# Joining the scan steps of a hybrid mixer block into fewer, longer visits between its projection products

## The chip, the cores and the metric

One Trainium2 chip, one core of it. The metric is device time in microseconds (us) of the one launch. TensorE (PE) multiplies, VectorE (DVE) and ScalarE (ACT) read and write PSUM and SBUF, GpSimd (POOL) reads and writes SBUF, and DMA queues are fed by SP, ACT and POOL.

## The reference

One layer over 512 latent tokens and 256 context tokens of width 2048, all in float32. Both streams are normalised, modulated by a condition, and multiplied by one wide input projection. Its columns feed three groups of heads: 6 heads of a bidirectional gated DeltaNet (GDN), a Hyena group of long convolutions, and 6 heads of a bidirectional mLSTM. The two scans, cut to their steps:

```python
# GDN, per chunk: dec = exp(g_i - g_j) below the diagonal
kk  = k @ k.T;  a_mat = I + tril(beta * kk * dec);  a_qk = (q @ k.T) * dec
def step(s):
    u = u_t - w @ s                       # the triangular solve is folded into u_t, w
    o = (q * exp(g)) @ s + a_qk @ u
    s = exp(g_end) * s + k_end.T @ u
# mLSTM, per chunk
p   = exp(d_log - m_i) * (q @ k.T)
num = w_inter * (q @ C) + p @ v;  den = w_inter * (q @ n) + p.sum()
h   = num / max(|den|, exp(-m_i));  C = dec * C + (w * k).T @ v
# every group: norm, gate, one output projection, residual, final norm
```

Each scan runs forwards and backwards; the latent scan starts from the state that the context scan leaves.

## The kernel before

The kernel works on tiles of 128 tokens: 2 context tiles and 4 latent ones, NT = 6 in all, NC_ = 2, NL = 4, and d = 0, 1 for the two directions. It has three stretches. The first loads, normalises and modulates the inputs and makes the Hyena filters. The middle one does the input projection, 64 column tiles of 128, with the scans between. The last does the long convolutions and the output projection.

The middle stretch is ordered by a planner written in Python, `weave` (from line 808). A *filling* generator yields one step of a projection product at a time, `product` (L396): three matmuls of 128x512 for the latent tokens (L404, L405, L409) and, for column tiles that need the context, three of 128x256 (L407, L408, L411). Weights are split into a high and a low part by ACT (L274) and DVE (L275), a few pieces ahead. Four *chains*, which are generators too, hold the rest: `gdn` (prepare and scan head after head), `ml_scans`, `gates_row` (a vector-matrix product on DVE, with its weights loaded by SP, L1535 and L1541) and, at the end, `convs`. A chain yields a pair: the planner's cost of the PE work that it has just issued, and a delay after which it is due again. Whenever a chain is due by the planner's clock, it gets a step; if none is due, the next product step is issued and the clock moves by 0.65 or 0.97. A stretch of chain steps between two product steps is called a *visit* here. The clock is a plan, not a measurement. The order so written is the priority of the instructions; the tile framework settles the final order on each engine from it when it is closed.

The steps that the change touches:

- `gdn_prep`, key products. For each tile t of six: one PSUM bank `pk` (tag "s", 2 banks), the product of the keys with themselves (L1305) and, for latent tiles, of the keys with the queries (L1307); then for both directions an exponential on ACT (`ex`, 2 buffers, L1310), a product into `M` on DVE (L1312) and one into `AT` (L1315). It yields after each tile with delay LX = 0.5. After the six, a visit of its own sums the squares of the queries (`pq`, L1325) and then `invert` starts: DVE, ACT and DMA work, with a wait on ACT's own DMA queue before the block `U32` is read back (L1158).
- `gdn_scan`. For each of six n, for both directions, in one PSUM bank `pp[d]` (tag "st", 3 banks): kT·S and `r` (L1356, L1358); a yield; M·r and `u` (L1363, L1365); a yield; ke·u and the new state `S` (L1372, L1377); a yield; for latent tiles the two output matmuls (L1385, L1386) into the same bank, read by ACT (L1389) and DVE (L1391, L1392); a yield of cost 0.88 and delay 0. The delays between are L1 = 0.6.
- `ml_scan`. Transposes of keys and values (L1455, copied by ACT, L1456); then for each of four latent tiles a bank of tag "s", the key-query product (L1467), two exponentials (L1470) and two products into `PT` (L1471), with a yield of delay LX after each tile; then twelve recurrent steps (L1485, L1488, L1489).

Of the kernel before, what the change touches and what calls it, by code (L numbers as in the profile page):

```python
# [10 lines left out]
F32 = mybir.dt.float32  # L11
# [4 lines left out]
ALU = mybir.AluOpType  # L16
# [5 lines left out]
CTX = 256  # L22
TOK = SEQ + CTX
NT = TOK // 128
NC_ = CTX // 128
NL = SEQ // 128
# [3 lines left out]
EPS = 1e-6  # L30
# [5 lines left out]
L1 = 0.6  # L36
# [3 lines left out]
LD = 3.5  # L40
LM = 0.5
LX = 0.5
LC = 6.0
LM0 = 1.0
LK = 8.0
# [178 lines left out]
def block_kernel(ctx: ExitStack, tc: tile.TileContext, io, out, dbg=None):  # L224
    nc = tc.nc
    PE, ACT, DVE, POOL, SP = nc.tensor, nc.scalar, nc.vector, nc.gpsimd, nc.sync
# [27 lines left out]
    def p_s():  # L254
        return bank("s", 2)
# [12 lines left out]
    ones = const.tile([128, 128], F32, name="ones")  # L268
# [177 lines left out]
    with ExitStack() as st:  # L446
# [23 lines left out]
        for k in range(KT):  # L470
# [11 lines left out]
            t = x_slot(F32)  # L482
# [112 lines left out]
        for k in range(KT):  # L595
# [6 lines left out]
            with tc.high_priority():  # L602
                for g in range(4):
                    G_ = slice(32 * g, 32 * g + 32)
                    i = PE.matmul(pa[G_], ones[:, 0:32], sqs[g], start=f, stop=l, tile_position=(0, 32 * g))
# [205 lines left out]
    clock = [0.0]  # L811

    def weave(chains, fill):

        chains = [[c, 0.0] for c in chains]
        filling = True
        while chains:
            for c in chains:  # L820
                if c[1]() if callable(c[1]) else c[1] <= clock[0]:
                    try:
                        y = next(c[0])
                    except StopIteration:
                        chains.remove(c)
                        break
                    if callable(y):
                        c[1] = y
                    else:
                        clock[0] += y[0]  # L830
                        c[1] = clock[0] + y[1]
                    break
            else:
                cost = next(fill, None) if filling else None
                if cost is None:
                    filling = False
                    clock[0] += 0.5
                else:
                    clock[0] += cost
        for _ in fill:  # L840
            pass
# [27 lines left out]
    with ExitStack() as st:  # L869
# [84 lines left out]
        for d in range(2):  # L954
# [18 lines left out]
            for n, t in enumerate(order):  # L973
# [3 lines left out]
                                       op0=ALU.add, op1=ALU.max)  # L977
# [273 lines left out]
    def gdn_prep(h, kT, vT, qT):  # L1251

        G = {}

        def rows(i):
            for d in range(2):
                g = s1.tile([128, 2, 128], F32, tag="G", bufs=GB, name="G")
                POOL.dma_start(out=g.rearrange("p t c -> p (t c)"),  # L1258
                               in_=rows_d[6 * d + h:6 * d + h + 1, 256 * i:256 * i + 256].to_broadcast([128, 256]))
                G[d, i] = g  # L1260

        def masks(i):
            for d in range(2):
                s_ = 1 if d == 0 else -1
                paced(POOL.affine_select(out=G[d, i], in_=G[d, i], pattern=[[0, 2], [s_, 128]], base=0,
                                         channel_multiplier=-s_, compare_op=ALU.is_ge, fill=-BIG))

        rows(0)
        rows(1)
        kt = s1.tile([128, NT, 128], F32, tag="kt", bufs=1, name="kt")  # L1270
        vr = s1.tile([128, NT, 128], F32, tag="vr", name="vr")
        ssk = s1.tile([128, NT], F32, tag="ssk", bufs=2, name="ssk")
        junk = s1.tile([128, 128], F32, tag="junk", bufs=1, name="junk")
        for t0, n in ((0, 4), (4, 2)):
            pt = p_s()
            for t in range(n):
                PE.transpose(pt[:, 128 * t:128 * t + 128], kT[:, 128 * (t0 + t):128 * (t0 + t) + 128], ident)
            DVE.tensor_copy(kt[:, t0:t0 + n], pt[:, :128 * n].rearrange("p (t c) -> p t c", c=128))
            for t in range(t0, t0 + n):
                ACT.activation(out=junk[:, :128], in_=kt[:, t], func=AF.Square, accum_out=ssk[:, t:t + 1])  # L1280
            yield 0.15 * n, 0.0
        DVE.tensor_single_scalar(out=ssk, in_=ssk, scalar=EPS, op=ALU.add)
        rk = s1.tile([128, NT], F32, tag="rk", bufs=2, name="rk")
        rsqrt(s1, rk, ssk, [128, NT], "rsq", 4)
        nk = s1.tile([128, NT], F32, tag="nk", bufs=2, name="nk")
        DVE.tensor_tensor(out=nk, in0=ssk, in1=rk, op=ALU.mult)
        DVE.tensor_tensor(out=rk, in0=rk, in1=rk, op=ALU.mult)
        dd = s1.tile([128, 2, NT], F32, tag="dd", bufs=2, name="dd")
        DVE.tensor_tensor(out=dd, in0=bet.rearrange("p t (d h) -> p d t h", d=2)[:, :, :, h],
                          in1=rk.unsqueeze(1).to_broadcast([128, 2, NT]), op=ALU.mult)  # L1290
        nd = s1.tile([128, 2, NT], F32, tag="nd", bufs=2, name="nd")
        DVE.tensor_single_scalar(out=nd, in_=dd, scalar=-1.0, op=ALU.mult)

        qsq = s1.tile([128, SEQ], F32, tag="yo", bufs=1, name="qsq")
        ACT.activation(out=qsq, in_=qT, func=AF.Square)
        yield 0, LK / 2
        masks(0)
        masks(1)
        yield 0, LK / 2
        MF = [s1.tile([128, NT, 128], F32, tag="big3", bufs=2, name="M") for _ in range(2)]  # L1300
        AT = s1.tile([128, 2, NL, 128], F32, tag="AT", bufs=1, name="AT")
        for t in range(NT):
            pk = p_s()
            kc = kT[:, 128 * t:128 * t + 128]
            PE.matmul(pk[:, 0:128], kc, kc, start=True, stop=True)  # L1305
            if t >= NC_:
                PE.matmul(pk[:, 128:256], kc, qT[:, 128 * (t - NC_):128 * (t - NC_) + 128], start=True, stop=True)  # L1307
            for d in range(2):
                ex = s1.tile([128, 128], F32, tag="ex", bufs=2, name="ex")
                ACT.activation(out=ex, in_=G[d, t // 2][:, t % 2], func=AF.Exp,  # L1310
                               bias=ngc[:, t, 6 * d + h:6 * d + h + 1])
                DVE.scalar_tensor_tensor(out=MF[d][:, t], in0=pk[:, 0:128], scalar=nd[:, d, t:t + 1], in1=ex,  # L1312
                                         op0=ALU.mult, op1=ALU.mult)
                if t >= NC_:
                    DVE.tensor_tensor(out=AT[:, d, t - NC_], in0=pk[:, 128:256], in1=ex, op=ALU.mult)  # L1315
            yield 0.22 if t < NC_ else 0.44, LX
            if t == 1:
                rows(2)
            if t == 3:
                yield 0, LD - 2 * LX  # L1320
                masks(2)
                yield 0, LX
        pq = p_s()
        for t in range(NL):
            PE.matmul(pq[:, t:t + 1], qsq[:, 128 * t:128 * t + 128], ones[:, 0:1], start=True, stop=True)  # L1325
        eq = s1.tile([128, NL], F32, tag="eq", bufs=2, name="eq")
        DVE.tensor_scalar(out=eq, in0=pq[:, :NL], scalar1=EPS, scalar2=128.0 * EPS, op0=ALU.add, op1=ALU.mult)
        yield 0.5, 0.0
        inv = invert(h, MF)
        yield next(inv)  # L1330
        for t0, n in ((0, 4), (4, 2)):
            pt = p_s()
            for t in range(n):
                PE.transpose(pt[:, 128 * t:128 * t + 128], vT[:, 128 * (t0 + t):128 * (t0 + t) + 128], ident)
            for t in range(n):
                ACT.activation(out=vr[:, t0 + t], in_=pt[:, 128 * t:128 * t + 128], func=AF.Copy,
                               scale=nk[:, t0 + t:t0 + t + 1])
            yield 0.15 * n, 0.0
        yield from inv
        if h == 0:  # L1340
            dump("F", MF[0].rearrange("p u c -> p (u c)"))
        return kT, qT, kt, vr, dd, eq, AT, MF

    def gdn_scan(h, kT, qT, kt, vr, dd, eq, AT, MF):
# [4 lines left out]
        for n in range(NT):  # L1349
# [17 lines left out]
            for d, t in enumerate(ts_):  # L1367
                if n + 1 < NT:
# [7 lines left out]
                    else:  # L1376
                        DVE.scalar_tensor_tensor(out=s[d], in0=S[d], scalar=gend[:, t, 6 * d + h:6 * d + h + 1],  # L1377
                                                 in1=pp[d][:, 256:384], op0=ALU.mult, op1=ALU.add)
            if n + 1 < NT:
                yield 0.44, L1  # L1380
            for d, t in enumerate(ts_):
                if t >= NC_:
                    j = t - NC_
# [10 lines left out]
                    if n >= 4:  # L1394
                        ACT.activation(out=junk[:, :128], in_=oo, func=AF.Square, accum_out=ss[:, j:j + 1])
            if n >= NC_:
                yield 0.88, 0.0
            S = s
        if h == 0:
            dump("o_gdn", o_sb.rearrange("p t c -> p (t c)"))  # L1400
# [40 lines left out]
    def ml_scan(h, kT, vT, qT, oT):  # L1441
# [21 lines left out]
        PT = s1.tile([128, 2, NL, 128], F32, tag="PT", bufs=1, name="PT")  # L1463
        for j in range(NL):
            t = j + NC_
            pk = p_s()
            PE.matmul(pk[:, 0:128], kT[:, 128 * t:128 * t + 128], qT[:, 128 * j:128 * j + 128], start=True, stop=True)  # L1467
            for d in range(2):
                ex = s1.tile([128, 128], F32, tag="ex", bufs=2, name="ex")
                ACT.activation(out=ex, in_=rows[d][:, j], func=AF.Exp, bias=am[:, t, 6 * d + h:6 * d + h + 1])  # L1470
                DVE.tensor_tensor(out=PT[:, d, j], in0=pk[:, 0:128], in1=ex, op=ALU.mult)  # L1471
            yield 0.22, LX
        o_sb = s1.tile([128, NL, 128], F32, tag="mosb", bufs=1, name="osb")
        Cn = [None, None]
        for n in range(NT):
# [367 lines left out]
```

## Time and profile before

| what | value |
|---|---|
| median of 3 runs (lowest, highest) | 1511.96 us (1509.89, 1512.82) |
| the profiled execution: its time, its span | 1511.28 us, 1509.5 us |
| PE busy | 1450.5 us, 96% |
| DVE, ACT, POOL busy | 1043.3, 575.8, 238.9 us |
| mean granted TensorE clock | 0.995 of full speed |
| matmuls in the trace | 8822 |

The span runs from the first to the last instruction; 1.78 us of the execution's time lie outside it. Matmuls are pipelined, and the profile models their ends, so a matmul's duration is longer than the distance to the next one. What the stream really costs is read from the distance between starts. PEld is the weight load that precedes a matmul; its waits show up before the matmul's own.

### The profile page before, as it was taken

The page shows a single profiled execution, that of the slowest core. Times are in us where ns is not written, and L with a number is a line of the kernel's source. Part 1 is how long each engine was busy: PE and PEld are TensorE (multiplying, and loading weights), DVE is VectorE, ACT ScalarE, POOL GpSimd, SP SyncE. Part 2 cuts the span into 40 slices and gives each one's busy share as a digit, 9 for nine tenths or more (in the row PEclk, how much of TensorE's full clock was granted, in tenths as well). Part 3 has the DMA queues.
Part 4 walks back from the last instruction along what each step waited for, and adds up shares of the span by engine and source line. Part 5 has one row for each costly group of instructions (what it writes and reads, how often), then busy time and mean ns, then how long its engine had stood idle before and what let it go on. Part 6 is the DMA issues. An engine that isn't in the chain of part 4 may idle for free.

```text
span 1509.5 us, 25117 instructions
## 1 busy us (share of the span) xinstructions
PE 1450.5 (96%) x8822; PEld 1187.7 (79%) x8822; DVE 1043.3 (69%) x2693; ACT 575.8 (38%) x1369; POOL 238.9 (16%) x428
## 2 busy tenths in 40 slices
PE   5898999999999999999999999999999999999996
PEld 1555687888888888878887888888878888888865
DVE  4567777676877777867777776677676676774455
ACT  6433433425242624253335333533353233332242
POOL 2224002102110211021102101200011121211111
PEclk9999999999999999999999999999999999999998
DMA  9987713233234423442344223311322543464343
GB/s 317 317 300 256 270 58 96 88 99 125 91 123 119 137 92 113 117 137 98 103 125 138 82 73 92 113 57 56 89 75 91 167 154 104 144 226 143 125 146 118
DMA packets 145237, 202.82 MB, mean 134 GB/s; under 512 B 57222, under 2 KB 57703, under 8 KB 144856
## 3 DMA queue, kind: packets, MB, share of 16 engines
q1 hardware_dynamic: 89752, 159.50, 31.8%
q0 software_dynamic: 10048, 32.52, 6.7%
q10 hardware_dynamic: 45312, 9.21, 3.2%
q8 instruction: 69, 1.13, 0.3%
q14 instruction: 56, 0.46, 0.1%
HBM read 182.92 MB, written 18.26 MB: 133 GB/s over the span
## 4 chain that ended last, share of the span: by engine, by line
PE 76%; DMA 9%; DVE 8%; issue 3%; ACT 2%; POOL 1%; SPq 0%; ACTq 0%; DVEq 0%; POOLq 0%
PE ml L404 13%; PE ml L405 13%; PE ml L409 13%; DMA mw<-in_mw_dram 4%; PE mc L407 3%; PE mc L408 3%; PE mc L411 3%; DVE wlo L275 2%; PE st L316 1%; PE st L1740 1%; PE st L1741 1%; PE st L1363 1%; PE st L1739 1%; DMA xs<-in_xT_dram 1%; DMA raw<-in_wo_dram 1%
## 5 line engine op out<-in xcount | busy, mean ns | idle before, releaser
L404 PE MATMUL ml<-xh,whi 128*128 128x512 f32 x1024 | 422.4, 413 | 0.0
L405 PE MATMUL ml<-xs,whi 128*128 128x512 f32 x1024 | 406.9, 397 | 0.0
L409 PE MATMUL ml<-xh,wlo 128*128 128x512 f32 x1024 | 404.4, 395 | 0.0
L274 ACT ACTIVATE whi<-raw 128x512 fp32r<-128x512 f32 x320 | 200.7, 629 | 492.0 <-PE mc L408 169.8
L275 DVE TENSOR_TENSOR wlo<-raw,whi 128x512 fp32r<-128x512 f32 x320 | 231.0, 724 | 184.4 <-ACT whi L274 179.6
L404 PEld LDWEIGHTS ml<-xh,whi 128*128 128x128 f32 x1024 | 193.1, 189 | 33.8 <-issue 1.7
L409 PEld LDWEIGHTS ml<-xh,wlo 128*128 128x128 f32 x1024 | 192.6, 188 | 24.8
L405 PEld LDWEIGHTS ml<-xs,whi 128*128 128x128 f32 x1024 | 193.4, 189 | 18.9
L407 PE MATMUL mc<-cs,whi 128*128 128x256 f32 x384 | 110.4, 288 | 0.0
L408 PE MATMUL mc<-cs,whi 128*128 128x256 f32 x384 | 108.7, 283 | 0.0
L411 PE MATMUL mc<-cs,wlo 128*128 128x256 f32 x384 | 107.8, 281 | 0.0
L408 PEld LDWEIGHTS mc<-cs,whi 128*128 128x128 f32 x384 | 72.3, 188 | 16.0
L407 PEld LDWEIGHTS mc<-cs,whi 128*128 128x128 f32 x384 | 72.1, 188 | 15.6
L411 PEld LDWEIGHTS mc<-cs,wlo 128*128 128x128 f32 x384 | 73.5, 191 | 0.0
L1541 DVE SCALAR_TENSOR_TENSOR gacc<-mg,scol,gacc 128x512 f32<-128x512 f32 x60 | 45.0, 750 | 24.9 <-DMA mg<-in_mg_dram 15.2
L1258 POOL DMA_DIRECT2D G<-rows_d x36 | 19.8, 551 | 222.4 <-DVE T L1124 75.5
L1248 POOL DMA_DIRECT2D yraw<-yo x12 | 7.0, 587 | 293.2 <-ACT yo L1247 218.1
L316 PE MATMUL st<-mw,s 128*32 128x512 f32 x256 | 35.5, 630 | 10.3 <-DMA mw<-in_mw_dram 8.9
L1789 POOL TENSOR_TENSOR res<-res,fnb 128x512 f32<-128x512 f32 x16 | 23.0, 1455 | 126.1 <-ACT xt L1788 126.1
L1483 POOL TENSOR_SCALAR ke<-kt,wend 128x128 f32<-128x128 f32 x60 | 26.7, 447 | 87.2 <-PE st L1485 43.5
L1740 PE MATMUL st<-wlo,yh 128*128 128x512 f32 x96 | 37.9, 398 | 2.7 <-DVE wlo L275 2.7
L1310 ACT ACTIVATE ex<-G,ngc 128x128 f32<-128x128 f32 x72 | 27.0, 398 | 32.7 <-DVE M L1312 11.1
(502 smaller groups left out, 2922.7 us busy)
## 6 DMA issues: line engine op xcount, KB each, us to landing
raw<-in_wt_dram SPq DMA_DIRECT2D x256, 256.0 KB, 2.8
mw<-in_mw_dram SPq DMA_DIRECT2D x128, 256.0 KB, 5.8
mg<-in_mg_dram SPq DMA_DIRECT2D x64, 256.0 KB, 2.8
raw<-in_wo_dram SPq DMA_DIRECT2D x64, 256.0 KB, 2.8
fraw<-in_wf_dram SPq DMA_DIRECT2D x16, 320.0 KB, 5.4
G<-rows_d POOLq DMA_DIRECT2D x36, 128.0 KB, 3.4
xs<-in_xT_dram SPq DMA_DIRECT2D x16, 256.0 KB, 5.6
hspec<-hv POOLq DMA_DIRECT2D x16, 256.0 KB, 4.7
```

Source lines behind the costliest of these rows:

```text
L274: ACT.activation(out=hi, in_=src, func=AF.Copy)
L275: DVE.tensor_tensor(out=lo, in0=src, in1=hi.bitcast(F32), op=ALU.subtract)
L316: i = PE.matmul(acc[32 * g:32 * g + 32], s32[:, 4 * g + j, :], mm[g], start=(j == 0), stop=(j == 3), tile_position=(0, 32 * g))
L404: PE.matmul(pl[:m], wh, xh[:, kk], start=f, stop=False)
L405: PE.matmul(pl[:m], wh, xl[kk], start=False, stop=False)
L407: PE.matmul(pc[:m, :CTX], wh, ch[kk], start=f, stop=False)
L408: PE.matmul(pc[:m, :CTX], wh, cl[kk], start=False, stop=False)
L409: stream[0] = PE.matmul(pl[:m], wl, xh[:, kk], start=False, stop=l)
L411: PE.matmul(pc[:m, :CTX], wl, ch[kk], start=False, stop=l)
L1310: ACT.activation(out=ex, in_=G[d, t // 2][:, t % 2], func=AF.Exp, bias=ngc[:, t, 6 * d + h:6 * d + h + 1])
L1541: paced(DVE.scalar_tensor_tensor(out=acc, in0=m, scalar=sk, in1=acc, op0=ALU.mult, op1=ALU.add))
L1740: PE.matmul(o, yh[k][:, ts_], wl, start=False, stop=False)
```

## The change

The planner gets one constant, LJ = 1.0: once a chain with PE work has run in a visit, every chain that has not yet run in this visit may run up to 1.0 ahead of its due time. The key products are made for two tiles at a time in one bank (GDN) or for all four latent tiles (mLSTM), with the exponentials and the DVE products for all of them behind, and one yield. The sums of squared queries move into the bank of the first key product. In the GDN scan the yield between the state update and the outputs goes, for latent tiles; the yield after the outputs gets the delay L1.

```diff
+LJ = 1.0
 ...
+        ran = []
         while chains:
             for c in chains:
-                if c[1]() if callable(c[1]) else c[1] <= clock[0]:
+                if c[1]() if callable(c[1]) else c[1] <= clock[0] + (LJ if ran and c not in ran else 0.0):
 ...
                         c[1] = clock[0] + y[1]
+                        if y[0]:
+                            ran.append(c)
                     break
             else:
+                ran = []
                 cost = next(fill, None) if filling else None
 ...
         for t in range(NT):
-            pk = p_s()
-            kc = kT[:, 128 * t:128 * t + 128]
-            PE.matmul(pk[:, 0:128], kc, kc, start=True, stop=True)
-            if t >= NC_:
-                PE.matmul(pk[:, 128:256], kc, qT[:, 128 * (t - NC_):128 * (t - NC_) + 128], start=True, stop=True)
+            if t % 2 == 0:
+                pb = p_s()
+                for i in range(2):
+                    kc = kT[:, 128 * (t + i):128 * (t + i) + 128]
+                    PE.matmul(pb[:, 256 * i:256 * i + 128], kc, kc, start=True, stop=True)
+                    if t >= NC_:
+                        j = t + i - NC_
+                        PE.matmul(pb[:, 256 * i + 128:256 * i + 256], kc, qT[:, 128 * j:128 * j + 128], start=True,
+                                  stop=True)
+            if t == 0:
+                pq = pb[:, 128:128 + NL]
+                for i in range(NL):
+                    PE.matmul(pq[:, i:i + 1], qsq[:, 128 * i:128 * i + 128], ones[:, 0:1], start=True, stop=True)
+                eq = s1.tile([128, NL], F32, tag="eq", bufs=2, name="eq")
+                DVE.tensor_scalar(out=eq, in0=pq, scalar1=EPS, scalar2=128.0 * EPS, op0=ALU.add, op1=ALU.mult)
+            pk = pb[:, 256 * (t % 2):256 * (t % 2) + 256]
 ...
-            yield 0.22 if t < NC_ else 0.44, LX
+            if t % 2:
+                yield 0.44 if t < NC_ else 0.88, 2 * LX
 ...
-        pq = p_s()
-        for t in range(NL):
-            PE.matmul(pq[:, t:t + 1], qsq[:, 128 * t:128 * t + 128], ones[:, 0:1], start=True, stop=True)
-        eq = s1.tile([128, NL], F32, tag="eq", bufs=2, name="eq")
-        DVE.tensor_scalar(out=eq, in0=pq[:, :NL], scalar1=EPS, scalar2=128.0 * EPS, op0=ALU.add, op1=ALU.mult)
-        yield 0.5, 0.0
 ...
-            if n + 1 < NT:
+            if n < NC_:
                 yield 0.44, L1
 ...
             if n >= NC_:
-                yield 0.88, 0.0
+                yield (1.32, L1) if n + 1 < NT else (0.88, 0.0)
 ...
-            pk = p_s()
-            PE.matmul(pk[:, 0:128], kT[:, 128 * t:128 * t + 128], qT[:, 128 * j:128 * j + 128], start=True, stop=True)
+            if j == 0:
+                pb = p_s()
+                for i in range(NL):
+                    PE.matmul(pb[:, 128 * i:128 * i + 128], kT[:, CTX + 128 * i:CTX + 128 * i + 128],
+                              qT[:, 128 * i:128 * i + 128], start=True, stop=True)
+            pk = pb[:, 128 * j:128 * j + 128]
 ...
-            yield 0.22, LX
+            if j == NL - 1:
+                yield 0.88, 4 * LX
```

## Rows read from the trace of the kernel before

**Rows 1.** Windows: stretch, length, busy us (instructions) by engine, clock, DMA share, GB/s.
```profile
0.00:245.00 245.00, 212.88 (x1191) 139.96 (x1192) 159.00 (x381) 106.28 (x209) 50.56 (x82) 0.99 0.69 237
245.00:1180.00 935.00, 926.15 (x6094) 789.09 (x6094) 677.35 (x1905) 364.03 (x956) 129.73 (x277) 1.00 0.34 102
1180.00:1510.00 330.00, 311.49 (x1540) 258.67 (x1538) 206.91 (x410) 105.47 (x204) 58.61 (x69) 0.99 0.45 149
```

**Rows 2.** Timeline around the third head's key products: start us, us, engine, instruction.
```profile
600.68 0.28 PE L411 MATMUL mc<-cs,wlo 128*128 128x256 f32 x1
...
601.03 0.40 PE L405 MATMUL ml<-xs,whi 128*128 128x512 f32 x1
...
601.73 0.28 PE L411 MATMUL mc<-cs,wlo 128*128 128x256 f32 x1
...
601.85 0.38 PE L1305 MATMUL s<-kT 128*128 128x128 f32 x2
...
602.07 0.39 PE L1307 MATMUL s<-qT,kT 128*128 128x128 f32 x2
...
602.53 0.39 PE L405 MATMUL ml<-xs,whi 128*128 128x512 f32 x1
...
603.28 0.35 DVE L1312 SCALAR_TENSOR_TENSOR M<-s,nd,ex 128x128 f32<-128x128 f32 x1
...
604.72 0.28 PE L411 MATMUL mc<-cs,wlo 128*128 128x256 f32 x1
...
604.83 0.95 PE L1325 MATMUL s<-ones,qsq 128*128 128x1 f32 x8
...
605.07 0.28 DVE L1315 TENSOR_TENSOR AT<-s,ex 128x128 f32<-128x128 f32 x1
...
605.96 0.39 PE L405 MATMUL ml<-xs,whi 128*128 128x512 f32 x1
```

**Rows 3.** Waits of the weight loads in 245:1180: us in total, times, longest.
```profile
PEld s L1455 <- ACT kt L1456: 8.7, 5, 3.1
PEld s L1467 <- DVE PT L1471: 2.9, 8, 0.5
...
PEld st L1356 <- DVE osb L1392: 1.4, 7, 0.3
...
PEld s L1325 <- DVE AT L1315: 0.9, 1, 0.9
```

**Rows 4.** Waits of the matmuls themselves in 245:1180.
```profile
PE s L1455 <- ACT kt L1456: 6.5, 4, 2.6
...
PE s L1325 <- DVE AT L1315: 0.5, 1, 0.5
```

**Rows 5.** Timeline of a state update and its outputs, fourth head.
```profile
862.31 0.45 PE L1372 MATMUL st<-u,ke 128*128 128x128 f32 x2
...
862.51 0.48 PE L404 MATMUL ml<-xh,whi 128*128 128x512 f32 x1
...
862.79 0.82 DVE L1377 SCALAR_TENSOR_TENSOR S<-S,gend,st 128x128 f32<-128x128 f32 x2 [0.17 <-PE st L1372]
...
862.82 0.40 PE L1372 MATMUL st<-u,ke 128*128 128x128 f32 x2
...
862.98 0.48 PE L405 MATMUL ml<-xs,whi 128*128 128x512 f32 x1
...
863.30 0.38 PE L1385 MATMUL st<-u,AT 128*128 128x128 f32 x2
```

**Rows 6.** Timeline where ACT waits for its own DMA, fourth head.
```profile
807.26 0.63 ACT L274 ACTIVATE whi<-raw 128x512 fp32r<-128x512 f32 x1 [4.07 <-DMA ublk<-R]
...
808.91 0.66 PE L1455 MATMUL s<-ident,vT 128*128 128x128 f32 x4 [2.62 <-ACT kt L1456]
```

**Rows 7.** Waits of all engines in 245:1180.
```profile
ACT whi L274 <- PE mc L408: 160.9, 65, 3.7
...
DVE gacc L1541 <- DMA mg<-in_mg_dram: 15.2, 15, 3.9
```

## The prediction

> **What bounds the kernel now.** I read the windows first. In the middle stretch, from 245 to 1180 us, PE is busy for 926.15 of 935 us at full clock, DVE for 677 and ACT for 364; all that the change edits lies in this stretch [rows 1]. The first stretch leaves PE idle for 32.1 us and the last for 18.5, and the edited steps issue nothing in either. So PE bounds the place of the change, and only two things can be won there: PE time that a visit costs beyond its own matmuls, and waits of PE inside visits. The timeline prices the first, the waits price the second. The table of waits shows little: the matmuls' own waits are led by 6.5 us of transposes behind ACT, and the loader's waits, which come earlier and are longer, by 8.7 us of the same [rows 3, 4].
>
> **What a visit costs.** Plain stream: from L411 to the next L405 it takes 601.03 - 600.68 = 0.35 us. With four scan instructions between them it takes 602.53 - 601.73 = 0.80, with eight 605.96 - 604.72 = 1.24 [rows 2]. Four instructions cost 0.45, eight 0.89, so one costs 0.11 and what is left for entering and leaving is 2 x 0.45 - 0.89 = 0.01 us. Times are given to 0.01, so it may be anything from 0 to 0.04. This is the number on which the case turns: joining visits is nearly worthless in itself.
>
> **Key products (a).** Per head GDN goes from seven stops (six tiles and the sums of squares) to three, and mLSTM from four to one; over six heads 42 stops go. The matmuls stay. 42 x 0.01 = 0.4 us is won, bounds 0 and 42 x 0.04 = 1.7.
>
> **Chains together (b).** LJ lets a waiting chain in up to 1.0 early. A product step moves the clock by 0.65 or 0.97, and the scans ask for 0.5 or 0.6, so they are due at every product step already; what can newly join are the five stops of an inversion, 30 over six heads. I take as much again as for (a), 0.4, bounds 0 and 30 x 0.04 = 1.2.
>
> **Waits that go (c).** The mLSTM products take turns on two banks, so the third and fourth wait until DVE has read the first two: 2.9 us in 8 waits of the loader. One bank for all four ends that. The sums of squares wait once for a bank, 0.9; they move into a bank that is free. The keys-times-state matmuls wait 1.4 us in 7 for the outputs' last read of the bank; now a product step lies between the two [rows 3]. Together 5.2 us by the loader. The loader waits ahead of the multiplier, so this is an upper bound; of these the matmuls' own waits show only the 0.5 [rows 4], the lower one. I take 2.9, the middle.
>
> **State and outputs (d).** In the GDN scan the number of stops does not fall: today the outputs and the next step's first matmuls are already one stop, as the delay between them is 0; afterwards the outputs stand with the state update instead. The joined outputs go into the bank from which DVE is reading the new state. In the rows the first state matmul starts at 862.31, DVE reads the state from 862.79 on, and the first output follows at 863.30 [rows 5]. That is 0.99 us after the state matmul, while the two state matmuls need 0.45: a hole of 0.54. It falls in three of the six n of each head, 18 times: 9.7 us if it stays open, 0 if it is filled. In the same rows two matmuls of the product, L404 and L405, stand in that hole, although neither a state update nor a product step yields in its middle: the program's final order already mixes a chain's matmuls with the product's where the chain must wait. The rows are thus near the filled end, and I take 1.0, bounds 0 and 9.7.
> The Trainium skill (PSUM — Partial Sum Buffer, Terms) says that TensorE writing and VectorE or ScalarE reading one bank on the same partitions at once is an error, which speaks against this join: by it alone each output would have to sit out the read, and the sum would carry the whole 9.7. The trace agrees as far as it goes, since no output in the rows starts before the first read is through; that the hole costs PE nothing is the rows' own addition.
>
> **Inversion later (e).** Today the last tile's products on DVE end at 605.07 + 0.28 = 605.35 [rows 2], and the inversion's DVE work starts behind. Joined, the last two tiles leave DVE four times 0.35 + 0.28, 2.5 us, behind a visit of eight instructions (0.89) that starts between 601.85, where the fifth tile's visit starts now, and 0.9 later, since the sums of squares now stand ahead of it. That ends between 605.2 and 606.2, so the inversion starts from 0.15 earlier to 0.85 later; I take 0.35. At its end ACT sits on its own queue until the inversion's DMA has landed (4.07 us in the fourth head), and the mLSTM transposes wait for ACT's copy, 2.62 us there [rows 6]. Five heads show such a wait [rows 3]. I count four at 0.35: 1.4 us lost, bounds -0.8 and 5 x 0.85 = 4.3.
>
> **Other queues (f).** The exponentials now come to ACT in fours and eights, ahead of weight splits. Those are covered: ACT mostly waits for PE to free a buffer before it can split (160.9 us on one product line alone), so the splits run ahead of need by whole pieces; without that cover each burst would cost PE its 2.5 us, 18 GDN and 6 mLSTM bursts, 60 us. The chain `gates_row` may be let in up to 1.0 earlier too, with its DVE step behind a load: 15 of its 64 steps wait for that load now, 15.2 us in all [rows 7]. What is queued behind is the scans' DVE work, for which PE waits. No scan matmul waits visibly for it today; I take 0.3, bounds 0 and 3.0 (a fifth of today's wait). No DMA is added or moved from one queue to another; POOL's state scaling stands where it stood.
>
> **The sum.** -0.4 (a) - 0.4 (b) - 2.9 (c) + 1.0 (d) + 1.4 (e) + 0.3 (f) = -1.0 us. The profiled execution took 1511.28, of which 1.78 lie outside its span, so 1510.3; that execution lies 0.68 below the median of the runs, 1511.96, so against the median 1511.0.
>
> **The rivals.** 0.2% is 3.0 us, about what a measurement of this kernel can tell from no change; the runs before span 2.9.
> - *No change that can be told* (forecast): 1511.0, by the sum. For it: a visit costs 0.01. That the change does not do what it says belongs here: if the program's order again puts product matmuls between the joined ones, as in [rows 5], (a) and (b) are 0 and the time stays near 1512. Chance 0.48.
> - *Faster*: the loader's waits all were PE's, the hole is filled for nothing, the inversion starts no later: -0.4 - 0.4 - 5.2 = -6.0, 1506.0. For it: those waits are in the table by name and the joined code has no cause for them. Against it: PE stands idle for 935 - 926.15 = 8.85 us in the whole stretch [rows 1], and without the transposes' 6.5 for 2.3. Chance 0.31.
> - *Slower, by the state's bank*: the hole stays open. -1.0 - 1.0 + 9.7 = +7.7, 1519.7. It decides from 1.0 + 1.0 + 3.0 = 5.0 us on, 0.28 us in each of 18 places. For it: DVE is busy 72% of the stretch, so the read may come later than in the rows. Against it: the product's matmuls that already fill it. Chance 0.15.
> - *Slower, by the inversion* at its bound of 4.3 with `gates_row` at 3.0: -1.0 + 2.9 + 2.7 = +4.6, 1516.6. Chance 0.06.
>
> **How the numbers follow.** Faster by over 0.2%: 0.31, the second case. Within: 0.48. Slower: 0.15 + 0.06 = 0.21. The time is that of the likeliest case, 1511.0; its own range is 1509 to 1515. The outer bounds are 1512 - 1.7 - 1.2 - 5.2 - 0.8 = 1503 and 1512 - 0.5 + 9.7 + 4.3 + 3.0 = 1528.5. Eight in ten: from 1505, a little below the faster case, as all its terms must be at their ends to pass it, to 1518, which leaves out most of the state's bank.
>
> **What would show it.** (a) The sums of squares stand right behind L1305 in one run, L1467 in six runs of eight, and the PE busy time of 245 to 1180 hardly moves. (c) The loader's waits of L1467, of the sums of squares and of L1356 are gone. (d) Between L1372 and L1385 stand product matmuls, and the loader of L1385 waits for the state for under 0.1 us each time; waits of 0.3 or more there, 18 of them, make the third case. (e) The transposes' wait for ACT is 0 to 4 us above 8.7. I am wrong if the middle stretch shortens by 5 us with the waits of [rows 3] unchanged: then a visit costs what the distances between starts don't show.

## The result and the profile after

The changed kernel takes 1523.09 us, median of four runs (1520.85 to 1524.83), beside 1510.93 for the kernel before in four runs (1509.02 to 1512.82): ratio 1.0070, 95% interval 1.0048 to 1.0091. It is slower by 0.7%, clear of the noise, and outside the range. Measured a second time it takes 1526.35 against 1513.47, 1.0075 (1.0052 to 1.0099). The profiled execution took 1524.57 us, its span is 1522.8, its mean clock 0.989.

The same three stretches as [rows 1], of after (length, then busy us and instructions of PE, PEld, DVE, ACT, POOL, then clock, DMA share, GB/s):

```profile
0.00:245.00 245.00, 215.78 (x1205) 142.47 (x1206) 161.93 (x392) 107.42 (x211) 51.35 (x82) 0.99 0.69 238
245.00:1180.00 935.00, 917.15 (x6027) 783.19 (x6026) 663.22 (x1871) 359.98 (x943) 127.57 (x277) 0.99 0.34 101
1180.00:1510.00 330.00, 321.51 (x1591) 268.23 (x1591) 208.75 (x411) 106.65 (x212) 57.29 (x68) 0.99 0.47 149
```

In the middle stretch PE is idle for 17.85 us, where it was 8.85, and has issued 67 matmul instructions fewer in the same 935 us. The loader's waits there, the rows that answer to [rows 3], and then the matmuls' own, which answer to [rows 4]:

```profile
PEld s L1468 <- ACT kt L1469: 15.1, 4, 5.9
...
PEld s L1482 <- ACT v L1469: 2.0, 1, 2.0
...
PEld s L1313 <- DVE AT L1333: 0.9, 1, 0.9
...
PEld st L1369 <- DVE osb L1405: 0.5, 3, 0.2
...
PEld st L1398 <- DVE S L1390: 0.4, 2, 0.2
```

```profile
PE s L1468 <- ACT kt L1469: 13.3, 4, 5.5
PE s L1482 <- ACT v L1469: 1.5, 1, 1.5
```

The eight waits of the mLSTM products for their bank are gone. The sums of squares no longer wait, but a key product now waits once for its bank, for the same 0.9 us (L1313). The wait for the outputs' last read fell from 1.4 to 0.5 us. The joined outputs wait for the state for 0.4 us in 2. The row that led before has grown most: the transposes' wait for ACT, from 6.5 to 13.3 us. The third head shows it. First before, on ACT (the queue's own instructions are marked ACTq) and PE:

```profile
644.90 0.55 ACTq L1155 DMA_DIRECT2D ublk<-R  x1
...
650.09 0.38 ACTq L1158 DMA_DIRECT2D U<-ublk  x1
...
652.25 0.66 PE L1455 MATMUL s<-ident,vT 128*128 128x128 f32 x4 [2.17 <-ACT kt L1456]
```

Then after, on ACT and on PE:

```profile
649.10 0.55 ACTq L1161 DMA_DIRECT2D ublk<-R  x1
649.77 0.63 ACT L275 ACTIVATE whi<-raw 128x512 fp32r<-128x512 f32 x1 [3.71 <-PE ml L410]
655.78 0.38 ACTq L1164 DMA_DIRECT2D U<-ublk  x1
656.29 0.63 ACT L275 ACTIVATE whi<-raw 128x512 fp32r<-128x512 f32 x1 [5.88 <-DMA ublk<-R]
...
657.30 0.86 ACT L1469 ACTIVATE kt<-s 128x512 f32<-128x512 f32 x2
```

```profile
651.53 0.48 PE L405 MATMUL ml<-xh,whi 128*128 128x512 f32 x1
651.85 0.40 PE L406 MATMUL ml<-xs,whi 128*128 128x512 f32 x1
652.08 0.40 PE L410 MATMUL ml<-xh,wlo 128*128 128x512 f32 x1
657.95 1.12 PE L1468 MATMUL s<-ident,vT 128*128 128x128 f32 x4 [5.47 <-ACT kt L1469]
658.71 0.78 PE L405 MATMUL ml<-xh,whi 128*128 128x512 f32 x1
659.29 0.63 PE L406 MATMUL ml<-xs,whi 128*128 128x512 f32 x1
```

ACT stores the inversion's blocks at 649.10 and may load U32 only when they have landed, at 655.78; the copies of the transposes stand behind that load in its queue, and PE stands for 5.47 us. After it, the distance from L405 to L406 is 0.58 us, where the first two rows, before the wait, are 0.32 apart. The windows of after say why (columns as above; the clock is the third number from the end):

```profile
640.00:652.40 12.40, 12.40 (x58) 9.78 (x56) 9.84 (x18) 1.90 (x3) 0.55 (x1) 1.00 0.45 126
652.40:657.90 5.50, 0.08 (x1) 0.00 (x0) 0.95 (x2) 1.61 (x4) 0.81 (x2) 0.83 0.54 127
657.90:662.80 4.90, 4.86 (x17) 4.17 (x18) 1.12 (x2) 1.78 (x5) 1.57 (x4) 0.50 0.54 163
662.80:680.00 17.20, 17.01 (x218) 14.61 (x217) 13.86 (x46) 13.05 (x43) 6.73 (x14) 1.00 0.45 139
...
816.40:823.20 6.80, 5.91 (x18) 3.58 (x19) 1.97 (x3) 2.96 (x7) 1.93 (x4) 0.50 0.43 105
```

The clock falls while PE still stands (0.83 in the mean of the second window), and for the next 4.9 us PE is busy at half of its clock, 1.2 of 2.4 GHz. The same comes in the fourth head at 816.40, and for 3.4 us from 499.0 in the second. Before has a clock of 1.00 behind its own waits of 2.17 and 2.62 us in the third and fourth heads:

```profile
652.30:657.00 4.70, 4.66 (x26) 3.69 (x27) 1.91 (x5) 3.18 (x9) 2.12 (x4) 1.00 0.50 172
...
809.00:816.00 7.00, 6.97 (x38) 5.48 (x39) 3.97 (x12) 5.11 (x15) 2.46 (x6) 1.00 0.41 133
```

The Trainium skill (TensorE: Matmul & The Clock Gate, HAM oscillation — how this bites in real kernels) describes this pattern, a wait of TensorE behind which the next tile starts at half clock; this trace agrees, with 0.50 behind the wait of 5.47 us.

So the loss can be booked. I take the time from the first matmul of the 9th column tile to that of the 58th, the same work in both, as it holds all the edited steps: 844.59 us before, 857.85 after. PE's idle time in it (no matmul running) is 8.85 and 17.85. Half of the time that PE was busy at half clock, an estimate of what that clock cost, is 0 and 7.11. That makes +9.0 and +7.1 of a difference of +13.3. The rest is -2.9; it has the sign of what the joins should save, but no row books it to them. Each side of this account is one execution.

### The profile page after: what moved, and what is told of

The parts are those of the page before. It is cut to its first block, busy times and chain, and to the rows that moved or that the text cites. A ratio compares the mean times of both kernels' runs of the same rounds, so it can differ in the third digit from the quotient of the medians.

```text
span 1522.8 us, 25078 instructions
## 1 busy us (share of the span) xinstructions
PE 1455.3 (96%) x8822; PEld 1194.2 (78%) x8822; DVE 1039.1 (68%) x2693; ACT 576.1 (38%) x1369; POOL 237.5 (16%) x428
## 4 chain that ended last, share of the span: by engine, by line
PE 75%; DVE 9%; DMA 6%; issue 5%; ACT 3%; POOL 1%; ACTq 0%; DVEq 0%; SPq 0%; POOLq 0%
PE ml L405 13%; PE ml L406 13%; PE ml L410 13%; PE mc L408 3%; PE mc L409 3%; PE mc L412 3%; DVE wlo L276 2%; PE st L1758 1%; PE st L1759 1%; PE st L1376 1%; PE st L1757 1%; PE st L317 1%; DMA mw<-in_mw_dram 1%; PE st L1385 1%; DMA raw<-in_wt_dram 1%
## 5 line engine op out<-in xcount | busy, mean ns | idle before, releaser
L405 PE MATMUL ml<-xh,whi 128*128 128x512 f32 x1024 | 421.4, 412 | 0.0
L406 PE MATMUL ml<-xs,whi 128*128 128x512 f32 x1024 | 406.5, 397 | 0.0
L405 PEld LDWEIGHTS ml<-xh,whi 128*128 128x128 f32 x1024 | 193.8, 189 | 32.7 <-issue 0.9
L406 PEld LDWEIGHTS ml<-xs,whi 128*128 128x128 f32 x1024 | 193.9, 189 | 19.7
L412 PE MATMUL mc<-cs,wlo 128*128 128x256 f32 x384 | 108.1, 282 | 0.0
L412 PEld LDWEIGHTS mc<-cs,wlo 128*128 128x128 f32 x384 | 73.5, 191 | 0.0
L1383 POOL TENSOR_SCALAR ke<-kt,kend 128x128 f32<-128x128 f32 x60 | 25.3, 425 | 174.2 <-PE st L1385 163.9
L1757 PE MATMUL st<-whi,yh 128*128 128x512 f32 x96 | 37.4, 396 | 1.4 <-ACT whi L275 1.4
```

Source lines behind the costliest of these rows:

```text
L405: PE.matmul(pl[:m], wh, xh[:, kk], start=f, stop=False)
L406: PE.matmul(pl[:m], wh, xl[kk], start=False, stop=False)
L412: PE.matmul(pc[:m, :CTX], wl, ch[kk], start=False, stop=l)
L1757: PE.matmul(o, yh[k][:, ts_], wh, start=f, stop=False)
```

## The experiments

Three theories stood at first. *Collision*: the change makes the inversion late against the mLSTM transposes, whose place behind the last mLSTM column tile is fixed (LM0), so that PE waits for ACT, and the clock falls behind the wait. *Bank*: the joined outputs wait for DVE's read of the state. *Phase*: any new order moves the steps against one another, and costs or gives a few us. All ratios stand in the table at the end of this section, each against runs of before that were taken beside it on the same chip.

**One part of the change alone.** Each kernel is before with one part of the change's diff: the GDN key products (`only_key`), state and outputs (`only_out`), the mLSTM key-query products (`only_ml`), LJ (`only_lj`).

> The kernel before with only the GDN key products joined (two tiles to a bank, sums of squares in the first). Collision theory: the inversion starts about 1 us later against the products, ACT sits in its own queue longer when the mLSTM transposes come, their wait for ACT grows from 6.5 us to over 10, PE drops to half clock behind it: 8 to 13 us slower than before, nearly all of the change's loss. Bank theory (the loss comes from outputs that wait for the state's read): within 2 us of before. Phase theory (any reorder shifts where the scan chain falls): a few us either way, and the parts do not add up to the whole.

> The kernel before with only the yield between state update and outputs taken out. Bank theory: 5 to 10 us slower, the loader of the first output matmul waiting for the state update 0.3 us and more in 18 places. Collision theory: within 2 us of before, no such waits. Phase theory: a few us either way with the transposes' wait for ACT moved.

> The kernel before with only the mLSTM key-query products joined into one bank. Collision theory: 0 to 3 us faster, as the loader's wait for the bank (2.9 us) goes and the joined products stand behind the transposes, so that they cannot delay them in the same head. Bank theory: the same. Phase theory: a few us either way.

> The kernel before with only the planner's early joining (LJ = 1.0). Collision theory: within 2 us of before. Bank theory: within 2 us. Phase theory: a few us either way, with the transposes' wait for ACT moved.

The bank theory falls: outputs joined alone measure 1.0009 (0.9994 to 1.0023), with no half clock in the middle and no wait of the outputs for the state among the loader's waits of 0.2 us and more. The mLSTM part is no different from nothing either. The loss comes from the keys (1.0026) and LJ (1.0040); alone on before, the four parts add up to 0.79%, about the whole. The keys lengthen the transposes' wait from 6.5 to 9.1 us, and at the two longest of these waits there is half clock, from 652 and 813 us. Half clock in one profile is not yet a loss, though: `only_ml` has 3.4 us of it by the account, and costs nothing that can be told. `only_lj` shows other waits than the collision's: the transposes' is down to 4.3, and new is one of the matmul that sums up `gacc`, the row of `gates_row`:

```profile
PE s L1550 <- DVE gacc L1547: 4.3, 2, 2.4
PE s L1461 <- ACT kt L1462: 4.3, 3, 1.8
PE s L1473 <- DVE PT L1477: 3.0, 3, 1.2
```

**Whom LJ lets in, and ACT's queue.** `lj_scans` and `lj_gates` are before with LJ for all chains but `gates_row`, and for it alone:

```diff
+        gates = chains[2]
 ...
-                if c[1]() if callable(c[1]) else c[1] <= clock[0]:
# lj_gates
+                if c[1]() if callable(c[1]) else c[1] <= clock[0] + (LJ if ran and c is gates else 0.0):
# lj_scans
+                if c[1]() if callable(c[1]) else c[1] <= clock[0] + (LJ if ran and c not in ran and c is not gates else 0.0):
```

`after_pool` and `before_pool` take the read-back of U32 off ACT's queue, after and before:

```diff
-            ACT.dma_start(out=U32, in_=ublk[h % 2].rearrange("u q r i -> (q r) u i"))
+            POOL.dma_start(out=U32, in_=ublk[h % 2].rearrange("u q r i -> (q r) u i"))
```

> The kernel before with LJ for the scan chains only; gates_row is never let in early. Theory A (the loss of LJ comes from gates_row: its DVE product, let in ahead of its load, holds DVE's queue and with it what PE waits for): within 2 us of before, no PE wait for gacc. Theory B (the scans' joined visits themselves cost, gates_row has nothing to do with it): the loss of only_lj stays, +4 to +7 us, with PE waits on kt and PT.

> The kernel before with LJ for gates_row only; the scans keep their due times. Theory A (gates_row let in ahead of its load): +3 to +7 us, with PE waits on gacc or PT of 3 us or more in the middle stretch and DVE's wait for mg above before's. Theory B (the scans' joined visits): within 2 us of before.

> The kernel after with the read-back of U32 issued by POOL, so that ACT no longer stands on its own queue until the inversion's blocks have landed. Theory C (the later inversion makes ACT late for the mLSTM transposes' copies, and the clock falls behind those waits): the transposes' wait goes from 13.3 to under 3 us, no half clock near 656 and 816 us, and the time falls by 5 to 9 us against after. Theory D (the transposes' wait costs little, the loss is spread over the joined visits): under 2 us.

> The kernel before with the same single move. It tells what the blocked ACT queue costs without the change: by theory C 3 to 7 us faster than before (its transposes wait 6.5 us); by theory D under 2 us.

Both halves of LJ cost about the same, 1.0026 and 1.0023, so neither A nor B holds as it was put. PE's wait for `gacc` does go with `gates_row`: 3.1 us in 2 in `lj_gates`, none in `lj_scans`. What LJ does to the inversion's start does separate them. I compare the end of the last `AT` product with that of before, less the shift of the product pieces around it: with the scans let in it moves by 0.0 to 0.13 us, with `gates_row` by up to 0.8; with the key join by 0.88 to 0.92 in each of the first five heads; in the changed kernel by +0.9, -2.3, +1.7, +1.3, +0.9 from the first head to the fifth.

`after_pool` gives back most of the loss (1.0014, from 1.0070, or 8.5 us), as C says, though the wait only halves, to 6.7 us, where C had under 3, and half clock stays, from 497 and 654 us. The same move is worth little in before (0.9988, interval to 1.0001): there C was too high.

**A later start of the mLSTM scan.** LM0 delays the transposes. `after_lm7_ng` also leaves `gates_row` out of LJ; `no_lj` is after without LJ.

```diff
-LM0 = 1.0
+LM0 = 7.0
```

> The kernel after with the mLSTM scan asked for 6 planner units later (LM0 = 7.0 for 1.0), so that its transposes come when ACT is long past the inversion's DMA. Theory C (the loss sits in the transposes' wait for ACT and the half clock behind it): the wait goes from 13.3 to under 3 us, no half clock between 490 and 830 us, time 6 to 11 us below after. Theory E (the wait only moves: something else is late by as much): within 3 us of after.

> The kernel before with the same one constant. Theory C: its own 6.5 us of that wait go, 3 to 7 us faster than before, and it stays 2 to 5 us ahead of after_lm7 by what gates_row loses. Theory E: within 2 us of before.

> after_lm7 with gates_row left out of LJ. Theory C with theory A (transposes and gates_row are together the whole loss): as fast as before_lm7 within 2 us. Theory B (the scans' joined visits cost in themselves): 3 to 5 us slower than before_lm7.

> The kernel after without LJ: key products and outputs joined, chains not. If LJ adds its 6 us to the rest independently: 1517 to 1519 us, 4 to 8 us below after, with the transposes' wait of 9 to 13 us still there. If the loss needs the parts together: within 2 us of before.

With the transposes six planner units later the whole loss is gone: 0.9999 (0.9983 to 1.0015), their wait down to 2.0 us, the clock at full speed all through the middle. That is C, and E falls for the changed kernel. For before it does not: it gains nothing (1.0014), though its wait falls from 6.5 to 1.5 us. There part of the wait only moves: the GDN transposes of the values (L1334) now wait 3.4 us for the same copies by ACT. By the account 3.8 us more of its middle are neither idle nor half clock, and what they are stays open; the rest of `after_lm7`, +0.3 where after has -2.9, is higher by about as much. `after_lm7_ng` is no faster than `after_lm7` (1.0016, 0.9999 to 1.0033) and as fast as `before_lm7`: with the transposes moved, `gates_row` in LJ costs nothing that can be told, and B falls. `no_lj` is the surprise: 1.0004 (0.9980 to 1.0027), with the key join in it.

**Once more, and both remedies together.** `after_again` is the changed kernel unedited, `after_ng` only keeps `gates_row` out of LJ; the other two have U32's load on POOL and LM0 = 4.0, with and without LJ.

> The changed kernel again, unedited, for a second profile. If the long waits for ACT recur: L1468 waits 10 us or more, half clock again behind the longest of them, 7 to 12 us above before. If the first profile was an odd one: a wait near 7 us and under 5 us above before.

> The changed kernel with gates_row left out of LJ, LM0 as it was. If LJ makes the transposes late through gates_row's DVE step: the wait falls from 13 to 8 us and the time by 4 to 7 us against after. If through the scans' own earlier steps: within 2 us of after.

> The changed kernel with both remedies: U32's read-back on POOL's queue and LM0 = 4.0. If the transposes' wait is the whole loss and the joins save what the rest of the account says (2 to 3 us): transposes' wait under 2 us, no half clock in the middle, 2 to 5 us below before. If a remedy only moves the wait: within 2 us of before.

> The same without LJ. If LJ still costs by itself: 2 to 5 us below after_pool_lm4 and 3 to 7 below before. If LJ costs only through the transposes: as after_pool_lm4 within 2 us.

The first profile was no odd one: the wait is 13.5 us again, with half clock at 659.4 and 816.4, and over its four runs the mean clock is 0.9878, where 20 runs of before have 0.9921. Taken as lost time that is 0.0122 of 1526 us against 0.0079 of 1513, a difference of 6.7 us; it is an upper bound for what the clock cost, as it counts time in which PE stood too. Without `gates_row` in LJ the loss falls from 0.75% to 0.22%, the wait to 9.3 us: most of what LJ adds comes through `gates_row`.

The start of the inversion is not all of it: the inversion also takes longer. From the end of `AT` to the load of U32 it is 42.8 and 44.7 us in the second and third heads of before, 46.0 and 46.5 in after, 43.3 and 44.0 in `after_ng`. In the second head of after the inversion starts 2.3 us earlier, and the wait of the transposes still grows from 0.4 to 2.5 us; 0.9 of that is a weight split that stands ahead of the copies in ACT's queue and waits for its own load (`raw`). In the fourth head the inversion takes no longer: 44.4 in before, 44.2 in after, 45.2 in `after_ng`.

`after_pool_lm4` contradicts C as it was put: the transposes wait for only 1.0 us, and yet it loses 0.32%. Its first rows of PE's waits, and then those of `no_lj_pool_lm4`:

```profile
PE s L1562 <- DVE gacc L1559: 3.0, 1, 3.0
PE st L1385 <- DVE u L1378: 2.5, 3, 1.3
PE s L1347 <- ACT v L1469: 2.5, 1, 2.5
PE s L1347 <- ACT kt L1469: 2.1, 1, 2.1
```

```profile
PE st L1379 <- DVE u L1372: 3.2, 5, 1.3
PE s L1462 <- ACT vr L1343: 2.4, 2, 2.3
PE s L1476 <- ACT vr L1343: 0.6, 2, 0.4
```

PE stands for `gacc` at 816 us and for the bank of L1347, the GDN transposes of the values, and half clock follows. L1347 waits 4.6 us for the same copies by ACT, so part of the transposes' wait has only moved. And `gates_row` let in early can also hold PE directly, as in `only_lj`. Without LJ the remedies and the other joins make the fastest kernel of the study: 1509.31 us in five runs, 0.9973 of before (0.9959 to 0.9986). Its transposes (L1462) wait no longer for the copies of the keys, but 2.4 us for a bank that ACT's copy of GDN's values still holds.

**What LJ and the keys need of one another.** `after_ng_pool_lm4` keeps LJ for the scans under both remedies; `no_key` is the changed kernel with the GDN key products tile by tile again.

> after_pool_lm4 with gates_row left out of LJ. If gates_row is what LJ costs: as no_lj_pool_lm4 within 2 us, that is 2 to 6 us below before, no PE wait for gacc of 1 us or more. If the scans' early steps cost as much: 2 to 5 us above no_lj_pool_lm4.

> The kernel after with the GDN key products tile by tile again, all else joined. If the key join and LJ add up: 5 to 8 us above before (0.35 to 0.55%), transposes' wait 5 to 8 us. If the loss needs both (a later inversion that gates_row delays further): within 3 us of before.

Keeping `gates_row` out takes 0.32% to -0.11% (0.9975 to 1.0003), most of the way to -0.27%. And `no_key` is at 1.0008 (0.9990 to 1.0027). Beside the other joins, then, the keys alone cost 0.04%, LJ alone 0.08%, neither to be told from nothing, and the two together 0.70 to 0.75%. On before alone the parts add up; taken out of the changed kernel, either one takes the whole loss with it. Costs that simply add cannot do both. That the two need one another fits a wait that grows once ACT is late enough, but for what each costs alone phase is not excluded.

The account uses the profiled execution, in us against before: idle, half clock and rest as in the section above. The wait is that of the transposes' own matmuls for ACT's copies of the keys (`kt`), in 245 to 1180; it is 6.5 in before and 13.3 in after. The medians are of ten runs, of four for `after_again` and five for `no_lj_pool_lm4`.

| kernel | median us | ratio to before (95%) | transposes' wait | idle, half clock, rest |
|---|---|---|---|---|
| only_key | 1517.00 | 1.0026 (1.0014, 1.0039) | 9.1 | +3.8, +3.2, -0.9 |
| only_out | 1513.09 | 1.0009 (0.9994, 1.0023) | 7.1 | +1.4, 0, 0.0 |
| only_ml | 1514.85 | 1.0004 (0.9985, 1.0024) | 7.1 | +1.5, +3.4, -1.9 |
| only_lj | 1518.77 | 1.0040 (1.0021, 1.0058) | 4.3 | +6.9, +1.7, +0.2 |
| lj_scans | 1516.45 | 1.0026 (1.0013, 1.0039) | 6.0 | +1.0, +3.4, -0.4 |
| lj_gates | 1516.57 | 1.0023 (1.0011, 1.0035) | 5.9 | +2.1, +3.4, 0.0 |
| after_pool | 1513.90 | 1.0014 (0.9999, 1.0029) | 6.7 | +3.5, +3.4, -2.2 |
| before_pool | 1510.03 | 0.9988 (0.9975, 1.0001) | 5.7 | 0.0, +1.7, -0.7 |
| after_lm7 | 1513.28 | 0.9999 (0.9983, 1.0015) | 2.0 | +2.4, 0, +0.3 |
| before_lm7 | 1514.45 | 1.0014 (0.9995, 1.0032) | 1.5 | +0.7, 0, +3.8 |
| after_lm7_ng | 1514.31 | 1.0016 (0.9999, 1.0033) | 1.3 | +1.9, 0, +1.5 |
| no_lj | 1514.70 | 1.0004 (0.9980, 1.0027) | 7.8 | +2.2, +2.9, -1.2 |
| after_again | 1526.35 | 1.0075 (1.0052, 1.0099) | 13.5 | +9.6, +4.0, -2.0 |
| after_ng | 1517.70 | 1.0022 (1.0010, 1.0035) | 9.3 | +5.6, +2.3, -1.7 |
| after_pool_lm4 | 1518.68 | 1.0032 (1.0017, 1.0047) | 1.0 | +5.0, +5.1, -2.5 |
| no_lj_pool_lm4 | 1509.31 | 0.9973 (0.9959, 0.9986) | 0 | -0.2, 0, -1.3 |
| after_ng_pool_lm4 | 1511.12 | 0.9989 (0.9975, 1.0003) | 0.5 | +1.6, +2.8, -1.4 |
| no_key | 1513.95 | 1.0008 (0.9990, 1.0027) | 6.3 | +1.8, +2.9, -1.3 |

## Why the prediction was wrong

**The step that failed is (e), the inversion later, together with the `gates_row` half of (f).** The fourth case, "slower, by the inversion at its bound of 4.3 with `gates_row` at 3.0", names the place; it got a chance of 0.06 and 4.6 us, where 12.2 were measured. Four things were mis-sized.

- *The lateness.* I took 0.35 us, with a bound of 0.85, for every head alike. The key join alone gives 0.88 to 0.92 in the first five heads, just past the bound, and LJ makes it anything from 2.3 us earlier (second head) to 1.7 later (third). The work behind the visit was right: from the last visit's end to the end of `AT` it is 2.4 us, where 2.5 was worked out. The start of that visit was not. These rows of after, of PE's matmuls and the last `AT`, answer to [rows 2]; the product piece that starts at 607.82 before starts at 610.06 here, 2.24 later.

```profile
605.90 0.28 PE L412 MATMUL mc<-cs,wlo 128*128 128x256 f32 x1
606.02 0.38 PE L1313 MATMUL s<-kT 128*128 128x128 f32 x2
606.24 0.39 PE L1316 MATMUL s<-qT,kT 128*128 128x128 f32 x2
606.46 0.39 PE L1313 MATMUL s<-kT 128*128 128x128 f32 x2
606.68 0.39 PE L1316 MATMUL s<-qT,kT 128*128 128x128 f32 x2
606.83 0.48 PE L405 MATMUL ml<-xh,whi 128*128 128x512 f32 x1
607.14 0.39 PE L406 MATMUL ml<-xs,whi 128*128 128x512 f32 x1
...
608.98 0.28 DVE L1333 TENSOR_TENSOR AT<-s,ex 128x128 f32<-128x128 f32 x1
```

 The visit begins 606.02 - 601.85 - 2.24 = 1.93 us later than the fifth tile's did; I had allowed 0 to 0.9. The sums of squares that now stand ahead make 0.88 of it, as in `only_key`. The other 1.05 is one product step: the visit stands behind the 365th, where before's fifth tile and `only_key`'s visit stand behind the 364th.
- *The inversion's length.* (e) let only the start of the inversion move and put its length at no change, without a reason. In the third head it goes from 650.09 - 605.35 = 44.7 to 655.78 - 609.26 = 46.5 us, so the 3.3 us by which PE's wait grows there are about half later start and half longer inversion. In the second head it goes from 42.8 to 46.0 us, more than the earlier start gives back.
- *What a wait costs.* I charged the transposes' wait us for us. It grew by 6.8 (bound 4.3), and the half clock behind the waits took another 7.1, which no term of mine held. The middle of before gave no hint of it, as its waits of up to 2.6 us there have none behind them; its first stretch did, with a clock of 0.51 from 46.3 to 53.2 us, around waits of PE of 2.4 and 1.3 us.
- *`gates_row`.* In (b) I said that LJ can newly let in only the inversion's stops. It also lets in `gates_row`, whose DVE step and matmul I priced at 0.3, bound 3.0, on the ground that no scan matmul waits visibly for them today. Keeping it out of LJ gives back 0.75 - 0.22 = 0.53%, 8 us. The comparisons show three ways: in some heads the inversion starts later, in some it takes longer, and PE waits for `gacc` itself.

**What held.** (a) A visit is nearly worthless in itself: around the joined visit above, from L412 to the next L406, it takes 607.14 - 605.90 = 1.24 us, and so eight key products in one stop cost what the eight sums of squares, of another shape, did before. The rest of the account is -1.2 to -2.9 us wherever several joins stand together and LM0 is 1.0 or 4.0, where (a) and (b) had 0.8 with bounds 0 and 2.9. The sums of squares do stand behind L1313 in one run. (c) Of the waits of [rows 3] for the banks L1467's are gone, L1356's are down to 0.5 us, and the 0.9 of the sums of squares passed to L1313; but that PE's idle time fell by 2.9 is not seen: in `only_ml` and `only_out` it is 1.5 and 1.4 above before's. Not even the lower bound, 0.5, shows. (d) The hole of the state's bank is filled, as taken. In the fourth head, to be held against [rows 5], L405 stands between the state update and the joined output:

```profile
873.25 0.46 PE L1385 MATMUL st<-u,ke 128*128 128x128 f32 x2
873.47 0.48 PE L405 MATMUL ml<-xh,whi 128*128 128x512 f32 x1
873.78 0.38 PE L1398 MATMUL st<-u,AT 128*128 128x128 f32 x2
```

Of the waits of 0.3 or more that I named as the mark of that case there is none. The mark of (e) did appear: the loader's wait for the transposes is 15.1 - 8.7 = 6.4 us above, outside the 0 to 4 that I gave.

**What stays open.** Why the key join alone costs 0.26% on before and 0.04% beside the other joins; the intervals overlap. Why LJ for the scans alone costs 0.26%, though it moves neither the inversion's start nor the transposes' wait; its profile has 3.4 us of half clock and 1.0 of idle, and its mean clock over ten runs is 0.9906, beside 0.9927 in 31 runs of before: as lost time 3.2 of the 3.7 us, at most. Why the inversion takes longer in the second and third heads of after, and not in the fourth. And whether DVE's or PE's part of `gates_row` does the harm, which no run separates.

## What to carry to other kernels

When a planner places steps by cost and delay, joining two steps moves every later step of that chain, and what counts is the one chain that it must meet at a fixed place: here the end of the inversion on ACT's queue and the transposes. Price a wait of the bounding engine at more than its length: here 9.0 us of new idle time came with 7.1 more at half clock. And a rule that lets work in early is safer without work whose data is still in flight: leaving `gates_row` out gave back 0.53% of the changed kernel, though nothing where the transposes came later.

## What the runs showed of the hardware

The length of a wait does not settle alone whether the clock falls. In the middle stretches of the 20 profiles, half clock began in, or within 2 us behind, all 7 of the waits of PE of 3.6 us and more, 3 of the 4 between 2.7 and 3.1, 14 of the 24 between 1.9 and 2.7, and none of the 35 between 1.2 and 1.9. Two waits of 2.16 us (in `lj_scans` and `after_pool`) were followed by half clock, before's of 2.17 was not. The stretches at half clock in the middle of after lasted 3.4 or 6.8 us. The clock also differs from execution to execution of one kernel: in the 31 runs of before beside `no_lj` the mean clock went from 0.989 to 0.996 and the time from 1507.13 to 1518.30, so before's own profile, at 0.995, showed a better than usual execution.

The queue of ACT is held by a load that waits for a store of its own: 5.88 us at 656.29 in after. The Trainium skill (TensorE: Matmul & The Clock Gate, Architectural detail) says that ACT and DVE take their instructions strictly first in, first out; for ACT the trace agrees, since the copies that PE waits for start only behind that load.
